# HGRN2 blocks half a period behind the RWKV blocks, in a two-layer encoder on one core

## The chip, the cores and the metric

One core of one Trainium2 chip. The metric is the device time of one execution, in microseconds; lower is better. Five engines work side by side, each through its own queue in order: TensorE (PE, matmuls), VectorE (DVE), ScalarE (ACT), GpSimd (POOL) and SyncE (SP, which issues all DMAs here).

## What is computed

Two layers over 2048 tokens of width 1024. The first mixes four HGRN2 heads ("a") and eight RWKV-7 heads of width 64 ("b"), the second is a convolution with an RG-LRU; each ends in a gated output projection and a layer norm.

```python
for l in range(DEPTH):
    mod = cond @ ada_w[l] + ada_b[l]
    shift, scale, gate = jnp.split(mod, 3, axis=-1)
    h = x * (1.0 + scale[:, None]) + shift[:, None]
    if l % 2 == 0:
        u = h @ ev_w_in[e]
        qA, fA, iA, gA, rB, kB, vB, zB, gB = jnp.split(u, EVEN_SPLITS, axis=-1)
        oA = hgrn2_chunkwise(qA, fA, iA, lbs[e], a_norm_g[e])
        oB, vf = rwkv7_mix(rB, kB, vB, zB, ...)
        mixed = jnp.concatenate([oA * jax.nn.silu(gA), oB * jax.nn.silu(gB)], axis=-1)
        y = mixed @ ev_w_out[e]
    else:
        ...
    x = layer_norm(DEEPNORM_ALPHA * x + (1.0 + gate[:, None]) * y, ln_g[l], ln_b[l])
```

The RWKV part is a scan with a state of 64x64 for each head:

```python
def step(S, inp):
    r_t, w_t, k_t, v_t, a_t, b_t = inp
    sa = jnp.einsum('bhvk,bhk->bhv', S, a_t)
    S = S * w_t[:, :, None, :] + sa[..., None] * b_t[:, :, None, :] + v_t[..., None] * k_t[:, :, None, :]
    return S, jnp.einsum('bhvk,bhk->bhv', S, r_t)
```

## The kernel before

The tokens go in two super-blocks of 1024, and each super-block through both layers. A projection is a product of 1024x128 weights with 2 x 512 tokens. Each factor is split in a high and a low part, so that every product is three matmuls (L431 to L433); the cast of the weights runs on ScalarE (L367), the low part on POOL (L368).

**mix0** (L1227) is the first layer's mixer, and the change lies in it. Its matmuls on TensorE come in an order that a small planner makes. One planner step is a quarter of a projection of 512 tokens, six matmuls. The generator `projections` gives these steps: the low-rank inputs, then for each of four groups g three RWKV and three HGRN2 projections, then the gates; it ends at step 272. The list `tasks` holds pairs of a due step and a generator. For each g and each half b of the super-block these are `rate_steps` (decay rates), `b_steps` (two RWKV heads over 512 tokens) at 40 + 48g + 24b, and `a_steps` (one HGRN2 head over the same tokens) at 64 + 48g + 24b. After each projection step every due task runs up to its next `yield n`, which makes it due n steps later. So a period is 24 steps, and in it one RWKV block and one HGRN2 block are woven into 24 steps of projections. This fixes TensorE's order only; the instructions of the other engines are put in order by a scheduler with priorities, and `tc.high_priority(offset=...)` puts some of them earlier.

**b_steps** has 8 chunks of 64 tokens in a block. In order:
- L857 to L894: normalised keys, decays, the products zr and bk;
- psc (L905, two groups of chunks) with its masks (L912, into the tile zb, called `sc` in the code): the score matrices;
- L918 and L921: the 16x16 diagonal blocks go out to DRAM and come back as ai, one block to a partition. L965 (POOL) writes the ones of the diagonal;
- pbn, pv, pk, pzt and pg: other products;
- L969 to L974 (VectorE): the inversion of the 16x16 triangles, 15 pairs of a multiplication and a sum; the result goes through DRAM again (L977, L980) into xd, and L984 transposes it into xn;
- plq (L994), pzq (L1004), plx (L1023) and pz (L1034): matmuls that join inverses of 16 into those of 64. Between pzq and plx stands a transposition on VectorE, xm (L1010), whose input ScalarE writes (L1008);
- pwv (L1049), pmq (L1063), and then the chain: pn (L1078), and for each of the eight chunks a pair of matmuls (L1087) with the state before, and a copy with decay on VectorE (L1090) that gives the next state. One chunk goes with each planner step;
- py and the group norm (pvr).

**a_steps** (L630) starts with a front: logarithms on ScalarE, then on VectorE L643, the scan L645, L647, L650 and the decay products L664 to L667; then the scores sc_a (L679), with L694 to put them into one tile, pk_a (L743), pst (L750), po_a and the normaliser pss_a (L785).

The block of a period and that of the next overlap: the chain of one RWKV block runs while the next block is inverted. `WO0` names the buffers of these blocks that hold the raw output weights when the blocks are through. `up` is the pool of the projections' outputs.

Of the kernel before, what the change touches and what calls it, by code (L numbers as in the profile page):

```python
# [31 lines left out]
INV_STEPS = 6  # L32
# [23 lines left out]
for _n, _w in VEC_FIELDS:  # L56
# [3 lines left out]
WO0 = (  # L60
    (1, "b_kk", 1), (1, "b_m1", 1), (1, "b_ep", 1), (3, "b_bk", 1), (1, "a_b", 1), (1, "a_e", 1), (1, "a_lf", 1),
    (1, "a_kz", 1), (2, "b_zg", 1), (2, "b_bkt", 1), (2, "b_sv", 2),
)
# [5 lines left out]
def tile_encoder(  # L69
# [19 lines left out]
    nc = tc.nc  # L89
# [10 lines left out]
    wp = ctx.enter_context(tc.tile_pool(name="wp", bufs=4))  # L100
    up = ctx.enter_context(tc.tile_pool(name="up", bufs=11))
    sp_ = ctx.enter_context(tc.tile_pool(name="sp", bufs=1))
# [741 lines left out]
    def b_steps(p, sb, b, us, sgi_of):  # L844
# [31 lines left out]
        lam = tp.tile([P, 8], F32, name=f"lam_{nm}", tag="b_lam", bufs=2)  # L876
# [21 lines left out]
        for c4 in range(2):  # L898
            yield (6, 2)[c4]
            pscs = [ps.tile([P, 4, P], F32, name=f"psc_{nm}_{hd}_{c4}", tag="tb", bufs=2) for hd in range(2)]  # L900
            for ci in range(4):
                for hd in range(2):
                    hs = slice(64 * hd, 64 * hd + 64)
                    c = c4 * 4 + ci
# [62 lines left out]
        for q in range(2):  # L967
            nc.gpsimd.memset(xt.rearrange("p n i -> p (n i)")[64 * q : 64 * q + 64, q:128:18], 1.0)
        for i in range(1, 16):  # L969
            n = i // 2 + 1  # L970
            pv_ = pr[:, 0 : n * (i + 1)].rearrange("p (n j) -> p n j", j=i + 1)
            av = ai[:, 0 : i + 1, i].rearrange("p (o j) -> p o j", o=1).broadcast_to([P, n, i + 1])
            nc.vector.tensor_mul(pv_, xt[:, 0:n, 0 : i + 1], av)
            nc.vector.tensor_reduce(out=xt[:, 0:n, i], in_=pv_, axis=AX.X, op=ALU.add)  # L974
        xd_dr = dram.tile([8, 8, 8, 2, 16], F32, name=f"xd_{nm}", tag="xd", bufs=2)
        for q in range(2):
# [9 lines left out]
        nc.gpsimd.tensor_copy(x32, xd)  # L986
        yield INV_STEPS

# [20 lines left out]
        xn = tp.tile([P, 8, 32], F32, name=f"xm_{nm}", tag="b_xn")  # L1009
        nc.vector.transpose(xn, x32)  # L1010
        tt = tt_tiles[tt_count[0] % 2]
        tt_count[0] += 1
        for hb in range(4):
            rs_ = slice(32 * hb, 32 * hb + 32)
            o_ = 32 * (hb % 2)
            nc.gpsimd.tensor_copy(tt[rs_, :, o_ : o_ + 32], x32[rs_])
        yield 2
        plx = ps.tile([P, 8, 32], F32, name=f"plx_{nm}", tag="tb", bufs=2)
# [65 lines left out]
        for c in range(8):  # L1084
            if states[c] is not None:
                for hd, hs in hds:
                    nc.tensor.matmul(  # L1087
                        pn[hs, c], sc[hs, 0, c, 0:64], states[c][hs], start=False, stop=True, skip_group_check=True
                    )
            nc.vector.tensor_scalar_mul(states[c + 1], pn[:, c], lam[:, c : c + 1])  # L1090
            yield 1
# [135 lines left out]
    def mix0(sb, hs, w_first):  # L1227
# [30 lines left out]
        for g in range(4):  # L1258
            for b in range(2):
                early = 4 if g == 3 and b else 0  # L1260
                tasks.append((34 + 48 * g + 24 * b - early, rate_steps(g, sb, b, lr, sgi_of)))
                tasks.append((40 + 48 * g + 24 * b - early, (g, b, b_steps, ub)))
                tasks.append((64 + 48 * g + 24 * b, (g, b, a_steps, ua)))

# [135 lines left out]
```

## Time and profile before

| | before |
|---|---|
| median of 3 runs | 2369.66 us (2367.89 to 2370.66) |
| profiled execution | 2367.25 us |
| its span | 2365.5 us |
| granted TensorE clock, mean | 0.969 of 2.4 GHz |
| TensorE busy | 2194.7 us (93%) |
| VectorE busy | 1455.6 us (62%) |
| ScalarE busy | 1264.6 us (53%) |
| POOL busy | 557.7 us (24%) |

TensorE's order is the program; where it has no work, an input is late. So the profile is read from TensorE's waits: which line waited, and which instruction of which engine it waited for. The granted clock is either 1.0 or 0.5 in a stretch (2.4 or 1.2 GHz), and a mean between the two says how much of a stretch ran at the lower. The first super-block's mixer runs from about 100 to 765 us, the second's from about 950 to 1575 us.

### The profile page before, as it was taken

The page shows a single profiled execution, that of the slowest core. Times are in us where ns is not written, and L with a number is a line of the kernel's source. Part 1 is how long each engine was busy: PE and PEld are TensorE (multiplying, and loading weights), DVE is VectorE, ACT ScalarE, POOL GpSimd, SP SyncE. Part 2 cuts the span into 40 slices and gives each one's busy share as a digit, 9 for nine tenths or more (in the row PEclk, how much of TensorE's full clock was granted, in tenths as well). Part 3 has the DMA queues.
Part 4 walks back from the last instruction along what each step waited for, and adds up shares of the span by engine and source line. Part 5 has one row for each costly group of instructions (what it writes and reads, how often), then busy time and mean ns, then how long its engine had stood idle before and what let it go on. Part 6 is the DMA issues. An engine that isn't in the chain of part 4 may idle for free. (4 is left out here: it accounts for less than half of the span.)

```text
span 2365.5 us, 45520 instructions
## 1 busy us (share of the span) xinstructions
PE 2194.7 (93%) x18400; PEld 1727.5 (73%) x18400; DVE 1455.6 (62%) x2697; ACT 1264.6 (53%) x2035; POOL 557.7 (24%) x586
## 2 busy tenths in 40 slices
PE   5989999999999999799999999899999999989998
PEld 4767777777777877577677777678777788767776
DVE  6546666667643678466675666436766556766366
ACT  4344655446666633445565456774467643666541
POOL 3311111212111322112111111112334331353321
PEclk7989999999999999899999999999999999999999
DMA  8210111111332637111111113326311564112652
GB/s 299 92 38 27 40 36 35 44 25 42 97 114 82 223 123 248 35 31 38 33 41 35 44 25 118 112 84 237 130 59 63 169 218 156 63 58 94 200 182 98
DMA packets 185938, 229.82 MB, mean 97 GB/s; under 512 B 65912, under 2 KB 99320, under 8 KB 185728
## 3 DMA queue, kind: packets, MB, share of 16 engines
q1 hardware_dynamic: 185728, 226.92, 30.1%
q8 instruction: 144, 2.36, 0.4%
q14 instruction: 66, 0.54, 0.1%
HBM read 175.46 MB, written 51.39 MB: 96 GB/s over the span
## 5 line engine op out<-in xcount | busy, mean ns | idle before, releaser
L431 PE MATMUL pp_g<-hl_h,wh_g 128*128 128x512 f32 x512 | 212.0, 414 | 4.0 <-ACT go L595 4.0
L433 PE MATMUL pp_g<-hh_h,wl_g 128*128 128x512 f32 x512 | 204.0, 398 | 4.0 <-POOL wl_g L368 4.0
L432 PE MATMUL pp_g<-hh_h,wh_g 128*128 128x512 f32 x512 | 204.4, 399 | 0.0
L368 POOL TENSOR_TENSOR wl_g<-raw_g,wh_g 128x512 fp32r<-128x512 f32 x64 | 97.5, 1528 | 349.9 <-ACT wh_g L367 307.8
L431 PE MATMUL po<-hl_wo,wh_mx 128*128 128x512 f32 x448 | 176.3, 393 | 4.0 <-DVE y L527 4.0
L433 PE MATMUL po<-hh_wo,wl_mx 128*128 128x512 f32 x448 | 175.4, 391 | 0.0
L432 PE MATMUL po<-hh_wo,wh_mx 128*128 128x512 f32 x448 | 174.9, 390 | 0.0
L431 PE MATMUL pp_b<-hl_h,wh_b 128*128 128x512 f32 x384 | 167.8, 437 | 5.1 <-ACT cr_b L838 5.1
L431 PE MATMUL pp_a<-hl_h,wh_a 128*128 128x512 f32 x384 | 168.9, 440 | 0.0
L432 PE MATMUL pp_b<-hh_h,wh_b 128*128 128x512 f32 x384 | 153.5, 400 | 0.0
L432 PE MATMUL pp_a<-hh_h,wh_a 128*128 128x512 f32 x384 | 153.4, 399 | 0.0
L433 PE MATMUL pp_a<-hh_h,wl_a 128*128 128x512 f32 x384 | 153.1, 399 | 0.0
L433 PE MATMUL pp_b<-hh_h,wl_b 128*128 128x512 f32 x384 | 152.7, 398 | 0.0
L368 POOL TENSOR_TENSOR wl_a<-raw_a,wh_a 128x512 fp32r<-128x512 f32 x48 | 66.9, 1402 | 329.0 <-ACT wh_a L367 329.0
L368 POOL TENSOR_TENSOR wl_mx<-raw_mx,wh_mx 128x512 fp32r<-128x512 f32 x64 | 80.8, 1268 | 255.7 <-ACT wh_mx L367 255.7
L368 POOL TENSOR_TENSOR wl_b<-raw_b,wh_b 128x512 fp32r<-128x512 f32 x48 | 67.4, 1409 | 269.1 <-ACT wh_b L367 260.0
L431 PEld LDWEIGHTS pp_g<-hl_h,wh_g 128*128 128x128 f32 x512 | 99.0, 193 | 27.8 <-ACT go L595 4.9
L433 PEld LDWEIGHTS pp_g<-hh_h,wl_g 128*128 128x128 f32 x512 | 99.0, 193 | 27.6 <-POOL wl_g L368 5.7
L587 DVE TENSOR_TENSOR go<-go,oi 128x512 f32<-128x512 f32 x64 | 45.9, 722 | 111.0 <-DMA oi<-o_dr 63.8
L432 PEld LDWEIGHTS pp_g<-hh_h,wh_g 128*128 128x128 f32 x512 | 99.4, 194 | 18.9
L433 PE MATMUL pp_c<-hh_h,wl_c 128*128 128x512 f32 x256 | 101.3, 397 | 11.0 <-POOL wl_c L368 9.6
L431 PE MATMUL pp_c<-hl_h,wh_c 128*128 128x512 f32 x256 | 101.6, 397 | 2.7 <-DVE hl_h L368 2.6
(355 smaller groups left out, 5677.8 us busy)
## 6 DMA issues: line engine op xcount, KB each, us to landing
adw<-in_ada_w_dram SPq DMA_DIRECT2D x96, 256.0 KB
oi<-o_dr SPq DMA_DIRECT2D x64, 256.0 KB
m_dr<-go SPq DMA_DIRECT2D x56, 256.0 KB
raw_b<-in_w_ev_dram SPq DMA_DIRECT2D x48, 256.0 KB
raw_a<-in_w_ev_dram SPq DMA_DIRECT2D x48, 256.0 KB
raw_g<-in_w_ev_dram SPq DMA_DIRECT2D x32, 256.0 KB
wo<-in_w_evo_dram SPq DMA_DIRECT2D x32, 256.0 KB
raw_mx<-m_dr SPq DMA_DIRECT2D x32, 256.0 KB
```

The costliest lines, as they stand in the source:

```text
L368: return (eng or nc.vector).tensor_tensor(out=lo, in0=src, in1=hi.bitcast(F32), op=ALU.subtract)
L431: nc.tensor.matmul(pt, ah, bl, start=first, stop=False)
L432: nc.tensor.matmul(pt, ah, bh, start=False, stop=False)
L433: nc.tensor.matmul(pt, al, bh, start=False, stop=last)
L587: nc.vector.tensor_mul(go[b], go[b], oi[b])
```

## The change

- `a_steps` are due 12 steps later, at 76 + 48g + 24b, half a period after where they were.
- `b_steps`: two steps more before plx (`yield 4`); xm and the chain's copies at high priority. The six steps that the inversion is given are now split, one before it, one after its ninth row, four behind it.
- the raw output weights go to buffers of the RWKV block only, since the last HGRN2 block still needs its own.
- 15 in place of 11 buffers for the projections' outputs, paid for with a smaller scratch (`dynamic_dma_scratch_size`).

```diff
-    (1, "b_kk", 1), (1, "b_m1", 1), (1, "b_ep", 1), (3, "b_bk", 1), (1, "a_b", 1), (1, "a_e", 1), (1, "a_lf", 1),
-    (1, "a_kz", 1), (2, "b_zg", 1), (2, "b_bkt", 1), (2, "b_sv", 2),
+    (1, "b_kk", 1), (1, "b_m1", 1), (1, "b_ep", 1), (3, "b_bk", 1), (2, "b_zg", 1), (2, "b_bkt", 1),
+    (2, "b_sv", 2), (2, "b_sv", 2), (1, "b_bv", 2), (1, "b_bv", 2),
...
-    up = ctx.enter_context(tc.tile_pool(name="up", bufs=11))
+    up = ctx.enter_context(tc.tile_pool(name="up", bufs=15))
...
+        yield 1
         for i in range(1, 16):
...
             nc.vector.tensor_reduce(out=xt[:, 0:n, i], in_=pv_, axis=AX.X, op=ALU.add)
+            if i == 9:
+                yield 1
...
-        yield INV_STEPS
+        yield INV_STEPS - 2
...
-        nc.vector.transpose(xn, x32)
+        with tc.high_priority(offset=300):
+            nc.vector.transpose(xn, x32)
...
-        yield 2
+        yield 4
         plx = ps.tile([P, 8, 32], F32, name=f"plx_{nm}", tag="tb", bufs=2)
...
-            nc.vector.tensor_scalar_mul(states[c + 1], pn[:, c], lam[:, c : c + 1])
+            with tc.high_priority(offset=300):
+                nc.vector.tensor_scalar_mul(states[c + 1], pn[:, c], lam[:, c : c + 1])
...
-                tasks.append((64 + 48 * g + 24 * b, (g, b, a_steps, ua)))
+                tasks.append((76 + 48 * g + 24 * b, (g, b, a_steps, ua)))
...
-    nc = bacc.Bacc("TRN2", target_bir_lowering=False, num_devices=1)
+    nc = bacc.Bacc("TRN2", target_bir_lowering=False, num_devices=1, dynamic_dma_scratch_size=1024)
```

Lines behind the inversion move by 3 to 5: L973 is L974 after, L974 is L975, L1010 is L1014, L1023 is L1027, L1087 is L1091, L1090 is L1095.

The order of VectorE before, in the second super-block, where the chain of one block (sb_b_1_1, the copies) meets the inversion of the next (pr_b_1_0); the numbers at the end of a name tell tiles apart:

```order
L1090 TENSOR_SCALAR sb_b_1_1_13005<-pn_b_1_1_13006,lam_b_1_1_11884 128x64
L912 TENSOR_TENSOR zb_b_1_0_12765<-psc_b_1_0_0_1_13027,bmask 128x512
L912 TENSOR_TENSOR zb_b_1_0_12765<-psc_b_1_0_1_1_13028,bmask 128x512
L1090 TENSOR_SCALAR sb_b_1_1_13005<-pn_b_1_1_13006,lam_b_1_1_11884 128x64 x2
L937 TENSOR_TENSOR b_bv_b_1_0_13092<-u_b_2_2_0_12514,pbn_b_1_0_13070 128x512
L1090 TENSOR_SCALAR sb_b_1_1_13005<-pn_b_1_1_13006,lam_b_1_1_11884 128x64 x2
L694 COPY_PREDICATED st_348<-lmask,sc_a_1_1_13113 64x4x8x4 x2
L694 COPY_PREDICATED st_348<-lmask,sc_a_1_1_13113 64x4x16x2 x2
L735 TENSOR_TENSOR a_kz_a_1_1_12676<-a_kz_a_1_1_12676,a_b_a_1_1_12674 128x4x64
L736 TENSOR_TENSOR u_a_1_1_11755<-u_a_1_1_11755,a_b_a_1_1_12674 128x4x64
L973 TENSOR_TENSOR pr_b_1_0_13230<-xt_b_1_0_13229,ai_b_1_0_13048 128x2
```

Copies 0 to 4 stand ahead of the first multiplication of the inversion (L973), with the score masks and the end of an HGRN2 block between them. The same place after, from copy 0 on:

```order
L1095 TENSOR_SCALAR sb_b_1_1_12941<-pn_b_1_1_12942,lam_b_1_1_11801 128x64
L937 TENSOR_TENSOR b_bv_b_1_0_13006<-u_b_2_2_0_12391,pbn_b_1_0_12984 128x512
L667 TENSOR_TENSOR w_a_1_1_12979<-w_a_1_1_12979,u_a_1_1_11682 128x8x32
L1095 TENSOR_SCALAR sb_b_1_1_12941<-pn_b_1_1_12942,lam_b_1_1_11801 128x64
L974 TENSOR_TENSOR pr_b_1_0_13144<-xt_b_1_0_13143,ai_b_1_0_12925 128x2
L1095 TENSOR_SCALAR sb_b_1_1_12941<-pn_b_1_1_12942,lam_b_1_1_11801 128x64
L975 TENSOR_REDUCE xt_b_1_0_13143<-pr_b_1_0_13144 128x1
L974 TENSOR_TENSOR pr_b_1_0_13144<-xt_b_1_0_13143,ai_b_1_0_12925 128x6
L975 TENSOR_REDUCE xt_b_1_0_13143<-pr_b_1_0_13144 128x2
L974 TENSOR_TENSOR pr_b_1_0_13144<-xt_b_1_0_13143,ai_b_1_0_12925 128x8
L975 TENSOR_REDUCE xt_b_1_0_13143<-pr_b_1_0_13144 128x2
```

The first multiplication (L974) now stands ahead of copy 2 (the third L1095), and the front of an HGRN2 block has passed already. A little further on in the same queue:

```order
L974 TENSOR_TENSOR pr_b_1_0_13144<-xt_b_1_0_13143,ai_b_1_0_12925 128x28
L975 TENSOR_REDUCE xt_b_1_0_13143<-pr_b_1_0_13144 128x4
L974 TENSOR_TENSOR pr_b_1_0_13144<-xt_b_1_0_13143,ai_b_1_0_12925 128x32
L975 TENSOR_REDUCE xt_b_1_0_13143<-pr_b_1_0_13144 128x4
L1095 TENSOR_SCALAR sb_b_1_1_12941<-pn_b_1_1_12942,lam_b_1_1_11801 128x64
```

Copy 3 stands behind the seventh pair. POOL's order at the same inversion before, with the memset of the diagonal (L965) between two low parts of weights:

```order
L368 TENSOR_TENSOR wl_a_2_1_13289<-raw_a_2_1_13286,wh_a_2_1_13288 128x512
L368 TENSOR_TENSOR wl_b_0_3_0_13540<-raw_b_0_3_0_13537,wh_b_0_3_0_13539 128x512
L965 MEMSET ai_b_1_0_13048 128x16
L368 TENSOR_TENSOR wl_b_0_3_1_13546<-raw_b_0_3_1_13543,wh_b_0_3_1_13545 128x512
L966 MEMSET xt_b_1_1_14089 128x128
```

And after:

```order
L368 TENSOR_TENSOR wl_a_2_0_13152<-raw_a_2_0_13149,wh_a_2_0_13151 128x512
L368 TENSOR_TENSOR wl_a_2_1_13158<-raw_a_2_1_13155,wh_a_2_1_13157 128x512
L965 MEMSET ai_b_1_0_12925 128x16
L368 TENSOR_TENSOR wl_b_0_3_0_13446<-raw_b_0_3_0_13443,wh_b_0_3_0_13445 128x512
L368 TENSOR_TENSOR wl_b_0_3_1_13452<-raw_b_0_3_1_13449,wh_b_0_3_1_13451 128x512
```

Of the two low parts of the projection b_0_3, one stood ahead of L965, and both stand behind it now. Last, VectorE at the transposition xm (L1010), before:

```order
L643 SCALAR_TENSOR_TENSOR a_lf_a_1_1_14384<-u_a_6_1_12887,a_e_a_1_1_14380 128x512
L645 SCALAR_TENSOR_TENSOR a_b_a_1_1_14386<-smask,a_lf_a_1_1_14384 128x512
L830 SCALAR_TENSOR_TENSOR u_b_2_3_1_14331<-pp_b_2_3_1_14262,vec,u_b_2_3_1_14331 128x511
L834 SCALAR_TENSOR_TENSOR u_b_2_3_1_14331<-cr_b_2_3_0_14230,vec,u_b_2_3_1_14331 128x1
L1010 STREAM_TRANSPOSE xm_b_1_1_14374<-x_b_1_1_14138 128x256
```

And after, where xm is L1014:

```order
L725 TENSOR_TENSOR u_a_1_1_11682<-u_a_1_1_11682,a_b_a_1_1_12969 128x512
L738 TENSOR_TENSOR dec_a_1_1_13497<-a_b_a_1_1_12969 128x4
L1122 SCALAR_TENSOR_TENSOR zb_b_1_1_11814<-py_b_1_1_13245,vec,zb_b_1_1_11814 128x512
L1123 SCALAR_TENSOR_TENSOR zb_b_1_1_11814<-zb_b_1_1_11814,vec,b_bv_b_1_1_12150 128x512
L1014 STREAM_TRANSPOSE xm_b_1_0_13433<-x_b_1_0_13223 128x256
```

The front of the HGRN2 block (L643, L645) stood ahead of xm; after, the end of the RWKV block before does (L1122 and L1123).

## Rows read from the trace of the kernel before

**Rows 1.** Stretches: us, busy per engine (instructions), granted clock, DMA share, GB/s; middles and tails.

```profile
190.00:612.00 422.00, 402.51 (x5017) 309.04 (x5012) 278.72 (x645) 229.25 (x426) 70.16 (x97) 0.98 0.13 37
612.00:765.00 153.00, 138.00 (x1461) 108.53 (x1460) 71.32 (x169) 98.75 (x153) 23.45 (x23) 0.93 0.35 103
...
1002.00:1427.00 425.00, 407.22 (x5119) 312.86 (x5118) 280.59 (x656) 233.86 (x431) 71.42 (x98) 0.99 0.14 37
1427.00:1575.00 148.00, 133.19 (x1445) 104.76 (x1445) 69.96 (x167) 93.21 (x147) 22.91 (x23) 0.92 0.33 99
```

**Rows 2.** TensorE's waits in the middles, first, then second: us in total, times, longest.

```profile
PE plx_b L1023 <- DVE xm_b L1010: 12.5, 5, 3.9
...
PE plx_b L1023 <- DVE xm_b L1010: 11.3, 5, 3.6
PE psc_b L905 <- DVE zb_b L912: 3.2, 6, 0.8
```

**Rows 3.** Timeline around one wait of plx: start, us, engine, line, operation, idle before.

```profile
1137.62 2.13 DVE L645 TENSOR_TENSOR_SCAN a_b_a<-smask,a_lf_a 128x512 f32<-128x512 bf16 x1
...
1138.09 1.08 ACT L1008 COPY x_b<-pzq_b 16x128 f32<-16x128 f32 x4
...
1141.48 0.43 DVE L1010 STREAM_TRANSPOSE xm_b<-x_b 128x256 f32<-128x256 f32 x1
...
1141.96 0.95 PE L1023 MATMUL plx_b<-xm_b,zb_b 32*32 32x32 f32 x32 [3.39 <-DVE xm_b L1010]
```

**Rows 4.** Stretches behind the wait of rows 3 and behind a wait of 1.63 us.

```profile
1142.20:1145.60 3.40, 3.40 (x35) 2.11 (x28) 1.76 (x4) 2.06 (x5) 0.12 (x1) 0.50 0.02 5
...
1070.00:1085.00 15.00, 13.73 (x168) 10.76 (x169) 12.42 (x27) 12.96 (x25) 2.70 (x7) 1.00 0.07 19
```

**Rows 5.** TensorE's waits in the second tail.

```profile
PE pst_a L750 <- ACT a_w_a L745: 3.3, 1, 3.3
PE sc_a L679 <- DVE w_a L667: 3.2, 1, 3.2
PE pwv_b L1049 <- ACT tt L1037: 3.0, 1, 3.0
PE plx_b L1023 <- DVE xm_b L1010: 2.7, 2, 1.9
...
PE pn_b L1087 <- DVE sb_b L1090: 0.9, 1, 0.9
```

**Rows 6.** Timeline of VectorE at one inversion in the second middle.

```profile
1240.25 1.29 DVE L912 TENSOR_TENSOR zb_b<-psc_b,bmask 128x512 f32<-128x512 f32 x2 [0.78 <-PE psc_b L905]
...
1253.29 0.15 DVE L973 TENSOR_TENSOR pr_b<-xt_b,ai_b 128x2 f32<-128x2 f32 x1
...
1253.67 0.17 DVE L973 TENSOR_TENSOR pr_b<-xt_b,ai_b 128x6 f32<-128x6 f32 x1
...
1256.44 1.30 DVE L973 TENSOR_TENSOR pr_b<-xt_b,ai_b 128x45 f32<-128x45 f32 x1
```

**Rows 7.** Instructions by line and shape on VectorE: busy us, mean ns, idle before.

```profile
L973 DVE TENSOR_TENSOR pr_b<-xt_b,ai_b 128x45 f32<-128x45 f32 x16 | 16.6, 1035 | 0.5
```

**Rows 8.** Timeline of POOL beside rows 6.

```profile
1250.20 1.27 POOL L368 TENSOR_TENSOR wl_b<-raw_b,wh_b 128x512 fp32r<-128x512 f32 x1 [16.67 <-ACT wh_b L367]
1251.42 0.13 POOL L965 MEMSET ai_b<- 128x16 f32 x1
1256.39 1.26 POOL L368 TENSOR_TENSOR wl_b<-raw_b,wh_b 128x512 fp32r<-128x512 f32 x1 [4.84 <-ACT wh_b L367]
```

**Rows 9.** Timeline of TensorE in a chain, before the inversion.

```profile
1173.01 0.33 PE L1087 MATMUL pn_b<-sb_b,zb_b 64*64 64x64 f32 x4
...
1174.86 0.33 PE L1087 MATMUL pn_b<-sb_b,zb_b 64*64 64x64 f32 x4
1175.12 1.12 PE L925 MATMUL pbn_b<-sgi,bones 128*128 128x512 f32 x2
...
1177.26 0.50 PE L431 MATMUL pp_b<-hl_h,wh_b 128*128 128x512 f32 x1
...
1182.51 1.02 PE L944 MATMUL pk_b<-ident,bk_b 64*128 64x64 f32 x16
```

## The prediction

> **What bounds the kernel now.** I read the table of stretches first [rows 1]. TensorE is busy for 2194.7 of 2365.5 us, so only what makes TensorE wait, or run at its lower clock, can move the time. The change touches mix0 alone, and there the table gives, for each super-block, a middle (six periods of 24 planner steps) and a tail (the last period and its drain). In the middles TensorE has 422.00 - 402.51 = 19.5 and 425.00 - 407.22 = 17.8 us without work, in the tails 15.0 and 14.8. The granted clock says the rest: 0.98 and 0.99 in the middles, 0.93 and 0.92 in the tails. A stretch at 0.5 loses half its length. The middles hold 13.6 and 10.2 us of such stretches, so 11.9 us lost in both; the tails lose 0.07 x 153 + 0.08 x 148 = 22.5 us.
>
> The waits say for what [rows 2, 5]. In the middles plx, the matmul behind the second transposition xm, waits 12.5 and 11.3 us, in five places each; in the second, psc, which needs a buffer back from the mask multiplication, adds 3.2 in six places. Smaller waits fill the rest. Two lines of the timeline show why [rows 3]: ScalarE has written the transposition's input at 1139.17, but VectorE has the front of the HGRN2 block in its queue, a scan of 2.13 us and three multiplications, and reaches L1010 only at 1141.48. The wait is 3.4 us, and behind it the clock is 0.50 for 3.4 us; behind a wait of 1.63 us it stays at 1.00 [rows 4]. So a long wait here costs half as much again.
>
> Sum before, to be replaced: middles 37.3 + 11.9 = 49.2 us (4.1 in each of 12 periods), tails 29.8 + 22.5 = 52.3 us. The two first blocks, before the middles, have the same TensorE order up to the first HGRN2 block, and I leave them as they are.
>
> **The change part by part.**
>
> *HGRN2 12 steps later; xm first; two steps more before plx.* In the new order the front of the HGRN2 block (L643 to L664) no longer stands between pzq and plx; xm follows the last two RWKV output instructions, and plx has two more quarter projections (2 x 1.59 us, from [rows 9]: 1.85 between two chain matmuls, less 0.26 for the pair itself) in front. What was 3.4 us late is then early by several us. I take all of plx's 23.8 us away. The waits of psc go too: in the new order its two groups are two steps away from pn and from the HGRN2 decay products. Between nothing and all of it, I take all, because xm's own work is 0.43 us [rows 3].
>
> *What is next: the state chain.* The chain pn -> copy -> pn of eight chunks has one copy on VectorE for each step. Before, copies 0 to 4 stand in VectorE's queue ahead of the small inversion of the next block, and its 30 instructions begin behind them. Now the first multiplication of the inversion stands ahead of copy 2, seven multiplication/sum pairs ahead of copy 3, three ahead of copy 4, and the rest with several HGRN2 decay instructions ahead of copies 5 and 6. High priority raised the copies, but not over these. VectorE works in order, so a multiplication that waits for its input holds the copy.
>
> When does that input come? Its chain is: last mask multiplication, eight stores, one load, POOL's L965. From the end of the mask multiplication for head 0 (1240.94, half of the pair at 1240.25 [rows 6]) to L965 it took 10.5 us [rows 8]; the change leaves this chain as it is. When does the chain need copy 2? Along TensorE from the end of the new psc (1.5 us ahead of that zero), by [rows 9]: two steps 2.93 (twelve matmuls in a row, somewhat less than twice 1.59), pn 1.0 (as pk), chain matmuls 0.26, pbn with pv 2.14 (1175.12 to 1177.26), step 1.59, 0.26, step 1.59, 0.26, pk 1.0, step 1.59: 12.6, so 11.1 us after zero.
>
> The first multiplication could go at 10.65. But POOL now has a low-part subtraction L368 right behind L965 (before, it stood ahead of it), and its cast is done by then: before, it let L368 start 9.3 us after the zero [rows 8]. Beside L368 the multiplication of 128x45 took 1.30 us, from 1256.44, when L368 ran from 1256.39; small ones alone take 0.15 to 0.17 [rows 6, 8]. So the first multiplication ends at about 11.9 and copy 2 at 12.2: TensorE waits 1.2 us. The six pairs that follow at 0.4 us each (1253.29 to 1253.67, [rows 6]) put copy 3 at 14.9, against a need of 12.3 + 1.85 = 14.1: a wait of 0.9 (1.0 with the semaphore). Copy 4 has the long step with pzt and pg in front and is on time. From there to copy 5 VectorE has five pairs and some eight HGRN2 instructions of 0.4 us, about 6.5 us from the end of the score matmul; this makes copy 5 late by about 1.8. With 0.4 for small ones: 4.35 us a period. The bounds: 0 where VectorE slips every copy in, and 7.2 where the second L368 falls on the pairs too and the clock falls (below).
>
> *The clock.* Two waits of 1.2 and 0.9 us within 3 us are between the wait of 1.63 that left the clock at 1.00 and that of 3.4 that halved it [rows 4]. I count a fall of 3.4 us (1.7 lost) in every second period: 0.85. Middles after: 12 x 5.2 = 62.4, which is 13 us more than before.
>
> *Tails.* The last HGRN2 block ends 12 steps later, beside the gate projections (which run to step 272), not further out. The tail's long waits [rows 5] come from the last RWKV and HGRN2 blocks being alone with little TensorE work between dependent steps. After: sc_a (3.2), pwv (3.0), pst (3.3) and plx (2.7) have their inputs ahead; new are pk_a behind L735, which now stands behind the bk products of the last RWKV block, at the price of sc_a, 3.2; the last normaliser sum pss_a behind a table load, at the price of pst, 3.3; and four late chain copies at the row's 0.9. Sum 10.1. Before, 11.2 us of clock were lost in each tail beside four waits of 1.9 to 3.3 us [rows 1, 5], 2.8 for each; two such waits remain, so about 5 us. Tails after: 2 x 15.1 = 30.2, a gain of 22 us. Bounds: 0 (a new long wait for each removed) to 40.
>
> *The rest at nothing.* Fifteen input tiles and the smaller scratch are space; no queue of POOL issues a DMA. The raw output weights take other buffers; their loads and the store of the last HGRN2 block now stand in another order on SP, ahead of out_proj, with the whole gate projection as cover; without it 1 to 2 us. Splitting the inversion's yield moves no matmul: between its pieces TensorE has nothing of this block.
>
> Sum: 13 - 22 = -9 against the profiled 2367.25 us; the median of the runs lies 2.4 above it, so 2369.66 - 9 = 2360 us.
>
> **The rivals.**
>
> *B: the multiplications are not held.* If the multiplication starts before L368, or POOL's cast is late, copy 2 is on time, copy 3 late by 0.9, copy 5 by 1.3, with 0.3 for small ones: 2.5 a period, 30 in all, -19 - 22 = -41: 2329 us. For it: POOL and VectorE are released at the same moment, since L965 frees both. Against it: L965 and L368 are neighbours on one queue, VectorE needs a semaphore in between, and before it was the multiplication that waited in 12 of 16 blocks (16.6 us in 16 [rows 7] is 12 of 1.30 and 4 of 0.25). The Trainium skill, "SBUF — State Buffer", section "Who interferes with whom", says that a VectorE instruction with two SBUF inputs and a GpSimd instruction that reads SBUF exclude each other for the whole instruction, and that issue order decides which blocks. By that rule the row of 1.30 us is an instruction that came second; one that comes first would cost nothing, and the time would be that of this rival.
>
> *C: the clock falls in every chain.* As forecast, but 1.7 us lost in all 12: 6.05 x 12 = 72.6, +23 - 22 = +1: 2371 us, no change to be measured. For it: the tails, where several waits lie close together, run at 0.92 [rows 1, 5]. Against it: a slower TensorE needs copy 5 later, which gives part back.
>
> *D: slower, the chain follows the inversion.* The place is copy 3 in each middle period. If the second L368 (15.5 us after zero before [rows 8]) comes before the seventh multiplication, that is before about 14.5, it holds a second multiplication: copy 3 is late by 2.2 instead of 0.9, every chain has more than 3 us of wait within 5 us, and the clock falls in each. 5.5 + 1.7 = 7.2 x 12 = 86.4, +37 - 22 = +15: 2385 us. The point is thus 1 us earlier than it was. For it: the casts follow the projections, and and the new period has less work between the two casts.
>
> **How the numbers follow.** Forecast 0.40, B 0.18, C 0.20, D 0.22. What a measurement of this kernel can tell from no change is about 0.2%, 4.7 us: 2365 to 2374. Faster: B and 0.32 of the forecast's own spread, 0.50. Same: 0.08 of the forecast and 0.13 of C, 0.21. Slower: D and 0.07 of C, 0.29. Range: from B's to D's time, 2328 to 2387; the forecast and C alone span 2350 to 2375.
>
> **What would show it.** In the changed trace: no wait of plx above 0.5 us; psc's 0.8 us waits gone; pn waiting for sb_b in about three places of each middle period, 1.2, 0.9 and 1.8 us, with a multiplication of over 1 us as the first of each inversion; the middles' idle time 50 to 55 us in place of 37.3; the tails' clock at 0.96 or 0.97. The prediction is wrong in its main step if pn's waits in the middles sum to under 15 us (then B or better) or if plx still waits. It is wrong on the tails if their idle time stays near 15 us each at a clock of 0.93.

## The result, and the profile after

The change makes the kernel slower: 2393.81 us median of 4 runs (2383.74, 2393.44, 2394.17, 2396.49) against 2368.77 us median of 4 runs of the kernel before, a ratio of 1.0094 (95% interval 1.0076 to 1.0112; the ratios here are estimates over all runs, so they need not be the quotient of two medians, 1.0106 in this case). The prediction was 2360 us, with a range up to 2387.

The profiled execution is the fastest of the four, 2383.74 us, 16.5 above the profiled one of before (2367.25). Its mean clock is 0.969, as before; the other three have 0.963 to 0.965, and (0.969 - 0.965) x 2390 is about 10 us, which is the step from 2383.74 to 2394. So the trace shows 16.5 of the 25 us; the rest stands in executions without a trace, and all that is known of it is their clock.

To place the 16.5 us, both traces are cut at the same matmuls: a middle from the first matmul of the projection of the second RWKV input in group 1 to the first gate projection, and a tail from there to the second output tile. The stretches first of before, then of after; the columns are the stretch, its length, busy time (and instructions) of PE, PEld, DVE, ACT and POOL, the granted clock, the DMA share and GB/s:

```profile
204.17:610.86 406.69, 388.06 (x4833) 297.02 (x4831) 264.32 (x619) 219.44 (x404) 67.41 (x95) 0.98 0.13 37
610.86:789.83 178.97, 163.07 (x1575) 128.92 (x1568) 88.46 (x193) 122.05 (x186) 31.79 (x30) 0.94 0.34 103
1020.66:1426.02 405.36, 388.52 (x4863) 297.53 (x4861) 265.07 (x627) 219.94 (x404) 67.67 (x95) 0.99 0.14 37
1426.02:1605.65 179.63, 163.88 (x1586) 129.83 (x1579) 88.35 (x193) 122.04 (x186) 30.80 (x30) 0.93 0.34 103
```

```profile
196.06:615.45 419.39, 391.27 (x4902) 300.12 (x4900) 259.55 (x621) 233.09 (x415) 60.48 (x95) 0.98 0.13 35
615.45:796.31 180.86, 165.47 (x1647) 132.21 (x1639) 98.38 (x205) 120.88 (x189) 31.08 (x30) 0.95 0.34 106
1023.14:1442.69 419.55, 391.53 (x4932) 301.26 (x4931) 260.16 (x629) 233.19 (x415) 60.54 (x95) 0.98 0.13 35
1442.69:1622.53 179.84, 165.37 (x1657) 132.26 (x1650) 97.81 (x205) 120.89 (x189) 30.14 (x30) 0.96 0.34 106
```

The middles are longer by 12.7 and 14.2 us, 27 in all. The tails are longer by 1.9 and 0.2. The parts ahead of the two middles are shorter by 8.1 and 4.0 us, since HGRN2 work has moved out of them: the counts of PE show some 70 more matmuls in each of the four stretches. In the middles TensorE now has 28.1 and 28.0 us without work, where it had 18.6 and 16.8. The waits of TensorE say for what; the columns are the line, what it waited for, us in all, how often, and the longest:

```profile
PE pn_b L1091 <- DVE sb_b L1095: 29.9, 17, 2.9
PE pzq_b L1007 <- ACT lq_b L1001: 14.1, 10, 1.6
PE plq_b L997 <- DVE xn_b L987: 13.0, 2, 6.9
...
PE pzt_b L955 <- ACT bkt_b L945: 10.1, 2, 5.2
PE pk_a L743 <- DVE a_kz_a L735: 7.3, 2, 3.7
PE po_a L774 <- DVE a_e_a L762: 6.9, 6, 1.2
```

The waits of plx and those of psc for zb [rows 2] are gone. In their place pn waits for the chain copy 29.9 us, pzq waits 14.1 us for a copy on ScalarE, and three smaller lines are new. (plq waits in the two first blocks, as before.)

**Where pn waits.** One meeting of chain and inversion in the second middle, first VectorE, then POOL, then TensorE; the columns are start, duration, engine, line, operation, output and inputs, and in brackets the idle time before and what ended it:

```profile
1189.19 0.16 DVE L974 TENSOR_TENSOR pr_b<-xt_b,ai_b 128x2 f32<-128x2 f32 x1 [3.82 <-POOL ai_b L965]
...
1189.64 0.88 DVE L974 TENSOR_TENSOR pr_b<-xt_b,ai_b 128x6 f32<-128x6 f32 x1
...
1192.47 0.94 DVE L974 TENSOR_TENSOR pr_b<-xt_b,ai_b 128x32 f32<-128x32 f32 x1
...
1193.55 0.27 DVE L1095 TENSOR_SCALAR sb_b<-pn_b,lam_b 128x64 f32<-128x64 f32 x1
```

```profile
1189.22 1.27 POOL L368 TENSOR_TENSOR wl_a<-raw_a,wh_a 128x512 fp32r<-128x512 f32 x1
1192.07 1.28 POOL L368 TENSOR_TENSOR wl_a<-raw_a,wh_a 128x512 fp32r<-128x512 f32 x1 [1.57 <-ACT wh_a L367]
```

```profile
1189.60 0.33 PE L1091 MATMUL pn_b<-sb_b,zb_b 64*64 64x64 f32 x4 [0.18 <-DVE xt_b L975]
...
1193.88 0.33 PE L1091 MATMUL pn_b<-sb_b,zb_b 64*64 64x64 f32 x4 [2.36 <-DVE sb_b L1095]
```

The first multiplication goes 0.03 us ahead of L368 and is not held (0.16), so copy 2, right behind it, makes TensorE wait 0.18 us only. The second is held by the first L368 (0.88 in place of 0.17), the seventh by the second L368 (0.94 in place of 0.21), and copy 3, queued behind it, makes TensorE wait 2.36 us. So it is in ten of the twelve inversions of the middles: the first multiplication leads L368 by 0.03 or 0.04 us and takes 0.16, and the second takes 0.88 to 0.96. In the other two L368 leads by 0.02 us, and the first takes 1.27 and 1.29. A later multiplication is held in all twelve (0.90 to 1.33), in ten of them ahead of copy 3, and in these ten TensorE waits 2.1 to 2.9 us for copy 3; in the other two it waits 1.2. This is where the Trainium skill, "SBUF — State Buffer", section "Who interferes with whom", agrees with the rows: of two instructions that exclude each other, the one that was issued later waits. (Whether the first multiplication put L368 off in turn, its 1.27 us do not show.)

**Where pzq waits.** ScalarE ahead of one such wait, and the wait on TensorE:

```profile
1210.51 1.28 ACT L819 ACT_TABLE_LOAD   x1
...
1213.30 1.28 ACT L666 ACT_TABLE_LOAD   x1 [0.80 <-DVE w_a L665]
...
1216.28 1.28 ACT L819 ACT_TABLE_LOAD   x1
...
1218.28 1.28 ACT L351 ACT_TABLE_LOAD   x1
...
1220.16 0.26 ACT L1001 COPY lq_b<-plq_b 128x128 f32<-128x128 f32 x1
```

```profile
1220.47 0.69 PE L1007 MATMUL pzq_b<-xd,lq_b 32*16 32x16 f32 x64 [1.49 <-ACT lq_b L1001]
```

L819 computes the two sigmoids of the decay rates. The exponentials of an HGRN2 block (L666) now stand between them, each function needs its table, and a load takes 1.28 us. The copy for pzq is queued behind. Over the whole kernel, first before, then after (a group's columns: count, busy us, mean ns):

```profile
L819 ACT ACT_TABLE_LOAD x16 | 20.5, 1283 | 0.3
```

```profile
L819 ACT ACT_TABLE_LOAD x26 | 33.4, 1283 | 0.5
...
L666 ACT ACT_TABLE_LOAD x16 | 20.5, 1283 | 8.1 <-DVE w_a L665 8.1
```

(L666 had 4 loads before; over all lines the kernel goes from 171 loads to 181.) For the middles the prediction did not read ScalarE's order.

### The profile page after: what moved, and what is told of

The parts are those of the page before. It is cut to its first block, busy times and chain, and to the rows that moved or that the text cites. A ratio compares the mean times of both kernels' runs of the same rounds, so it can differ in the third digit from the quotient of the medians.

```text
span 2382.0 us, 45521 instructions
## 1 busy us (share of the span) xinstructions
PE 2191.5 (92%) x18400; PEld 1729.3 (73%) x18400; DVE 1456.3 (61%) x2697; ACT 1283.9 (54%) x2045; POOL 543.0 (23%) x586
## 4 chain that ended last, share of the span: by engine, by line
PE 53%; DVE 21%; ACT 10%; DMA 7%; issue 5%; SPq 2%; POOL 1%; DVEq 0%; POOLq 0%; ACTq 0%
PE po L431 4%; PE po L433 4%; PE po L432 4%; DMA ai_b<-ad_b 3%; PE pp_g L431 3%; PE pp_g L432 3%; PE pp_g L433 3%; DVE pr_b L974 3%; PE pp_a L431 2%; PE pp_b L431 2%; PE pp_b L432 2%; PE pp_b L433 2%; PE pp_a L432 2%; PE pp_a L433 2%; DVE xc_c L1148 2%
## 5 line engine op out<-in xcount | busy, mean ns | idle before, releaser
L368 POOL TENSOR_TENSOR wl_g<-raw_g,wh_g 128x512 fp32r<-128x512 f32 x64 | 96.5, 1512 | 309.9 <-ACT wh_g L367 304.8
L368 POOL TENSOR_TENSOR wl_mx<-raw_mx,wh_mx 128x512 fp32r<-128x512 f32 x64 | 81.6, 1277 | 273.0 <-ACT wh_mx L367 214.2
L974 DVE TENSOR_TENSOR pr_b<-xt_b,ai_b 128x2 f32<-128x2 f32 (+14 forms) x240 | 80.9, 337 | 64.4 <-POOL ai_b L965 58.0
L432 PE MATMUL pp_c<-hh_h,wh_c 128*128 128x512 f32 x256 | 100.6, 393 | 0.0
```

The costliest lines, as they stand in the source:

```text
L368: return (eng or nc.vector).tensor_tensor(out=lo, in0=src, in1=hi.bitcast(F32), op=ALU.subtract)
L432: nc.tensor.matmul(pt, ah, bh, start=False, stop=False)
```

## The experiments

After the result three theories of the loss stood: that the chain copies stand behind the inversion in VectorE's queue, and it is held by POOL; that the parted sigmoids hold ScalarE; and, against the first, that copies put ahead only move the loss, since the inversion then starts later. The first runs tell these apart; each edit is on top of the changed kernel unless it says otherwise.

### Copies ahead of the inversion

The first multiplication of an inversion is issued only after the newest chain copy:

```diff
-            nc.vector.tensor_mul(pv_, xt[:, 0:n, 0 : i + 1], av)
+            if i == 1 and last_copy[0] is not None:
+                with tc.issue_after(last_copy[0]):
+                    nc.vector.tensor_mul(pv_, xt[:, 0:n, 0 : i + 1], av)
+            else:
+                nc.vector.tensor_mul(pv_, xt[:, 0:n, 0 : i + 1], av)
...
+                cp = nc.vector.tensor_scalar_mul(states[c + 1], pn[:, c], lam[:, c : c + 1])
+            last_copy[0] = cp.ins
```

> The changed kernel, but the first multiplication of each small inversion is put in VectorE's order behind the newest chain copy, so that copies 0 to 4 stand ahead of it, as they did before the change. Theory 1 (the copies that wait behind the inversion and its multiplications, with the falls of the clock behind them, are the largest part of the loss): pn's waits for its copy, 29.9 us in 17 places in the changed kernel, drop below 6 us, the middles' clock returns to 0.98 to 0.99, and the time falls by 25 to 40 us, to 2355 to 2370. Theory 2 (the extra loads of ScalarE's tables and the waits of pzq behind them): pzq's 14.1 us stay, and the time falls by less than 10 us. Theory 3 (what the chain gains the inversion loses, which starts later): plq then waits for xn in the middles, 1 to 3 us in each of 12 periods, and the time stays within 10 us of the changed kernel's 2394.

Measured: 2402.49 us, 1.0142 [1.0117, 1.0167] against before: slower than the change itself. The waits of its TensorE:

```profile
PE plq_b L1002 <- DVE xn_b L992: 77.8, 16, 9.5
...
PE pn_b L1096 <- DVE sb_b L1100: 0.8, 2, 0.4
```

The chain's 29.9 us are down to 0.8, and plq, behind the inversion, now waits in all 16 blocks: 64.8 us more. For this edit the last of the three holds: the wait moves. Why plq waits, VectorE's order shows:

```profile
1204.80 0.15 DVE L977 TENSOR_TENSOR pr_b<-xt_b,ai_b 128x2 f32<-128x2 f32 x1
```

In the middles six copies (0 to 5) now stand ahead of the first multiplication, one more than before the change, and it starts 18.9 to 22.2 us after the score masks' zero (1185.69 here), in place of 10.4 to 11.8 in the change. VectorE is not full there: in the 7.4 us ahead of 1200.09 it has three copies of 0.28 us and otherwise waits for pn. So this edit does not show that there is no room for both; an order between the two, with copy 2 or 3 ahead, was not tried.

### The two sigmoids side by side

```diff
-        for i, bias in enumerate(("w0", "a0")):
-            last = nc.scalar.activation(sgi[:, i], pws[i], AF.Sigmoid, bias=V(bias, p))
+        first = nc.scalar.activation(sgi[:, 0], pws[0], AF.Sigmoid, bias=V("w0", p))
+        with tc.issue_after(first.ins), tc.high_priority():
+            last = nc.scalar.activation(sgi[:, 1], pws[1], AF.Sigmoid, bias=V("a0", p))
```

> The changed kernel, but the two sigmoids of each rate step stand next to each other on ScalarE, so that no exponential of an HGRN2 block comes between them. Table loads in front of L819 and L666, 26 and 16 in the changed kernel against 16 and 4 before, should return to about 16 and 6. Theory 2 (the table loads delay lq, so that pzq waits): pzq's waits, 14.1 us in ten places, drop below 3 us, and the time falls by 10 to 20 us, to 2374 to 2384. Theory 1 (chain copies): a fall of at most 10 us, since pn's 29.9 us stay. If the plq result waits for ScalarE for another reason, pzq's waits stay above 8 us.

Measured: 2372.61 us, 1.0017 [1.0004, 1.0029]: 21.2 us less than the change. The waits of pzq are gone, the loads at the sigmoids are back at 16, and those at L666 are 6:

```profile
L818 ACT ACT_TABLE_LOAD x16 | 20.5, 1283 | 0.3
...
L666 ACT ACT_TABLE_LOAD x6 | 7.7, 1283 | 1.1 <-DVE w_a L665 1.1
```

So ScalarE's order is worth 21 us of the change's loss, the term that the prediction lacked. Between the profiled executions it is 14.6 us (2369.15 at a clock of 0.974): pzq's 14.1 are gone, while pn's waits, with those put down to the inversion's sums, go from 30.9 to 35.0, and pzt's 10.1 stay.

### Both orders

The two edits together.

> Both edits: copies ahead of the inversion, and the two sigmoids together. If both causes are real and stand one behind the other on TensorE's path, the gains add: 2340 to 2355, faster than the kernel before. If the waits replace one another (theory 3), it is no faster than the better of the two by more than 5 us, and stays above 2362.

Measured: 2404.43 us, 1.0151 [1.0128, 1.0174]; plq waits 75.4 us in 15 places. With the copies first, the inversion is late whatever ScalarE does; pzq's waits are gone with that edit alone, and the sigmoids' gain does not show.

### The diagonal on VectorE

POOL's L965 goes to VectorE. POOL's L368 then need not wait for it and can run before the inversion, and the first multiplication no longer waits for POOL to write the diagonal:

```diff
-        nc.gpsimd.memset(ai.rearrange("p s t -> p (s t)")[:, 0:256:17], 1.0)
+        nc.vector.memset(ai.rearrange("p s t -> p (s t)")[:, 0:256:17], 1.0)
```

> The changed kernel, but the ones on the diagonal of ai are written by VectorE in place of POOL, so that POOL's low parts (L368) are no longer queued behind that load. The first one then runs as soon as its cast is done, some 2 us before the inversion starts, and the multiplication of 128x6, 0.88 us beside it in the changed kernel, takes about 0.17. If POOL's hold on VectorE is what makes copy 3 late, pn's longest waits, 2.36 us in the middles, drop to 1.3 to 1.7, and the time falls by 8 to 20 us (with fewer falls of the clock). If only the order counts (the copies behind seven pairs), they stay above 2 us and the time within 6 us of 2394.

Measured: 2374.92 us, 1.0025 [1.0012, 1.0037]: 18.9 us less than the change. The same meeting as above, POOL, then VectorE, then TensorE:

```profile
1177.95 1.29 POOL L368 TENSOR_TENSOR wl_a<-raw_a,wh_a 128x512 fp32r<-128x512 f32 x1 [19.88 <-ACT wh_a L367]
1182.93 1.26 POOL L368 TENSOR_TENSOR wl_a<-raw_a,wh_a 128x512 fp32r<-128x512 f32 x1 [3.70 <-ACT wh_a L367]
```

```profile
1180.50 0.17 DVE L974 TENSOR_TENSOR pr_b<-xt_b,ai_b 128x6 f32<-128x6 f32 x1
...
1182.97 0.27 DVE L1095 TENSOR_SCALAR sb_b<-pn_b,lam_b 128x64 f32<-128x64 f32 x1
1183.16 1.12 DVE L974 TENSOR_TENSOR pr_b<-xt_b,ai_b 128x45 f32<-128x45 f32 x1
```

```profile
1183.30 0.33 PE L1091 MATMUL pn_b<-sb_b,zb_b 64*64 64x64 f32 x4 [0.92 <-DVE sb_b L1095]
```

The first L368 runs before the inversion, the second multiplication takes 0.17, and the one that is held comes behind copy 3, which is late by 0.92 in place of 2.36. So the hold decides 1.4 us of copy 3's 2.36, and the seven pairs in front of it the other 0.9. (The inversion starts 10.9 us after the masks' zero in both meetings; in all twelve of the middles the second multiplication now takes 0.16 or 0.17.) The chain's waits fall from 29.9 to 22.8, the longest from 2.9 to 1.7. The profiled execution is 6.7 us shorter (2377.06); the median falls by 18.9. The rest stands in executions without a trace, and goes with the clock: 0.971 to 0.974 in all ten executions of this kernel, against 0.963 to 0.965 in three of the change's four.

### Both remedies, and three priorities more

Sigmoids and diagonal together, and then with the state updates of the HGRN2 block, its L735 and the bkt copies ahead as well:

```diff
+        with tc.high_priority(offset=300):
             nc.vector.tensor_mul(v128(ke)[:, :, 0], v128(ke)[:, :, 0], end(1).broadcast_to([P, 4, 64]))
...
+        with tc.high_priority(offset=300):
             for j in range(3):
                 state_after(j)
...
+            with tc.high_priority(offset=300):
                 nc.scalar.copy(bkt[:, hd], pk)
```

> The changed kernel with the two edits that each took some 20 us off: the sigmoids of a rate step next to each other, and the diagonal's ones on VectorE. If the two causes are independent (pzq behind ScalarE's table loads, copy 3 behind the multiplications that POOL holds), their gains of 21.2 and 18.9 us add, but for the clock that both give back: 2348 to 2360, faster than the kernel before by 0.4 to 0.9%. If both had acted on the same lost time, 2365 to 2373.

> The same two edits, and high priority for the HGRN2 state updates (L762), for the decay product in front of pk_a (L735) and for the copies of bkt on ScalarE. po_a waits for L762 6.9 us in six places of the changed kernel; these should fall below 2 us, so 4 to 8 us less than with the two edits alone. pk_a's 7.3 us and pzt's 10.1 us stand in the tails, where the order hardly moves: they should stay above 10 us in sum. If the tails' waits move as well, 10 to 16 us less.

Measured: 2354.72 us, 0.9948 [0.9924, 0.9971], for the two; 2329.41 us, 0.9833 [0.9810, 0.9856], with the priorities. The two gains add up: 21.2 + 18.9 = 40.1, and 2393.81 - 2354.72 = 39.1. The priorities give 25.3 more, where I had expected 4 to 8, or 10 to 16 if the tails moved too. po_a's and pk_a's waits (6.9 and 7.3) are gone, pzt's 10.1 stays; by the cuts at the same matmuls the two tails are 12.4 us shorter in all than with the two edits alone and the two middles 9.4, and the tails' clock is 0.98 and 0.97 in place of 0.96 and 0.95. Which of the three priorities did it was not tried. What is left of the chain's waits is many short ones, at a clock of 0.975 in the profiled execution:

```profile
PE pn_b L1095 <- DVE sb_b L1099: 19.9, 22, 1.7
```

This is the fastest kernel of the study, and it keeps the change's own order of TensorE, the two steps ahead of plx included.

### The parts of the change one by one

The shift alone: the kernel before with HGRN2 blocks due 12 steps later, the raw output weights' buffers, 15 input tiles and the smaller scratch, but no step added, no priority and no split. And xm's priority alone, on the kernel before:

```diff
-                tasks.append((64 + 48 * g + 24 * b, (g, b, a_steps, ua)))
+                tasks.append((76 + 48 * g + 24 * b, (g, b, a_steps, ua)))
```

```diff
-        nc.vector.transpose(xn, x32)
+        with tc.high_priority(offset=300):
+            nc.vector.transpose(xn, x32)
```

> The kernel before with the half-period shift of the HGRN2 blocks alone (with the buffers that it needs), no priorities, no split of the inversion and plx still two steps behind pzq. In its order copies 0 to 2 stand ahead of the inversion, copy 3 behind six pairs. Theory A (the shift as such brings the new waits: chain copies behind the inversion and POOL's low parts, pzq behind ScalarE): the time is 2375 to 2400, near the changed kernel's, and pn waits 15 us or more. Theory B (the shift alone gains, and the two priorities and the split, which pull the inversion ahead of copy 2, do the harm): 2340 to 2362, pn's waits under 10 us, plx's gone.

> The kernel before with the high priority for the transposition xm alone. In its order xm moves by at most a few instructions and still stands behind the scan of the HGRN2 block, because priorities decide only between instructions that the scheduler takes to be ready. If that is right, plx keeps its 29.1 us of waits (25 to 30) and the time is within 6 us of 2369. If the priority moves xm to where its input is ready, plx's waits fall below 12 us and the time to 2340 to 2355.

Measured: the shift alone 2336.08 us, 0.9873 [0.9840, 0.9907]; xm's priority alone 2369.64 us, 1.0002 [0.9984, 1.0019]. Priority did not help xm: plx still waits 28.3 us in 13 places (29.1 in 14 before). The shift clears plx by itself. Its waits, in a trace of the slowest of its four executions (2349.14 at a clock of 0.965; the others, 2335 to 2337, have 0.971 and 0.972):

```profile
PE pn_b L1087 <- DVE sb_b L1090: 11.5, 8, 3.2
PE pzq_b L1004 <- ACT lq_b L998: 8.5, 3, 3.0
PE plx_b L1023 <- DVE dec_a L738: 7.7, 2, 4.0
...
PE plx_b L1023 <- DVE xm_b L1010: 2.7, 2, 1.3
```

What is left of plx is four waits in all, in the tails. So the change holds something that costs 58 us more than its own main part, and the candidates are the two steps before plx, the priorities and the split. (I had expected the priorities and the split to do the harm.)

### The two steps before plx

The change with its two extra steps taken away, and the shift alone with only these two steps added:

```diff
-        yield 4
+        yield 2
         plx = ps.tile([P, 8, 32], F32, name=f"plx_{nm}", tag="tb", bufs=2)
```

```diff
-        yield 2
+        yield 4
         plx = ps.tile([P, 8, 32], F32, name=f"plx_{nm}", tag="tb", bufs=2)
```

> The changed kernel with one number put back: two steps, not four, between pzq and plx. The chain then runs two steps earlier against the inversion of the next block. In VectorE's order copies 0 to 2 stand ahead of the first multiplication again and copy 3 behind six pairs; the two sigmoids are parted in 3 places, not 10. If these two steps are the whole difference between the shift alone (2336) and the change (2394), the time is 2330 to 2350, pn waits under 15 us and pzq under 9 us. If the priorities or the split do the harm, it stays above 2370.

> The kernel before with the shift and the four steps ahead of plx, without the priorities and without the split of the inversion. Its order on VectorE, ScalarE and POOL shows the same pattern as the changed kernel's (first multiplication ahead of copy 2, seven pairs ahead of copy 3, sigmoids parted in 10 places). If the two steps are the cause, it is as slow as the changed kernel: 2383 to 2400, pn waits 25 to 35 us, pzq 12 to 16. If the priorities or the split are, it is near the shift alone, 2335 to 2350.

Measured: the change without the two steps 2343.36 us, 0.9876 [0.9855, 0.9897]; the shift with them 2393.93 us, 1.0096 [1.0076, 1.0116], the time of the change (1.0094). So the two steps alone turn a gain of 1.2% into a loss of 1%: 50.4 us with the priorities and the split (2393.81 against 2343.36), 57.8 without them (2393.93 against 2336.08). The priorities and the split do nothing clear of the noise: 0.1 us with four steps, and with two 7.3 us slower, where the intervals overlap almost wholly (0.9876 and 0.9873). The long waits of the shift with four steps are those of the change, within 2 us a line:

```profile
PE pn_b L1087 <- DVE sb_b L1090: 31.9, 18, 2.9
PE pzq_b L1004 <- ACT lq_b L998: 14.0, 10, 1.8
...
PE pzt_b L955 <- ACT bkt_b L945: 10.1, 2, 5.2
```

And the meeting of chain and inversion on VectorE in the change without them:

```profile
1163.79 0.28 DVE L1095 TENSOR_SCALAR sb_b<-pn_b,lam_b 128x64 f32<-128x64 f32 x1 [1.56 <-PE pn_b L1091]
1165.87 0.16 DVE L974 TENSOR_TENSOR pr_b<-xt_b,ai_b 128x2 f32<-128x2 f32 x1 [1.80 <-POOL ai_b L965]
...
1167.80 0.27 DVE L1095 TENSOR_SCALAR sb_b<-pn_b,lam_b 128x64 f32<-128x64 f32 x1
...
1168.91 1.08 DVE L974 TENSOR_TENSOR pr_b<-xt_b,ai_b 128x45 f32<-128x45 f32 x1
```

The chain is two steps earlier against the next block, and copies 0 to 4 stand ahead of the inversion, as before the change. A copy stands 2 us ahead of the first multiplication here, VectorE still idles 1.8 us before it, the next copy goes behind five pairs in time, and the multiplication that is held (1.08) comes behind that. In the second middle pn waits 3.7 us in four places, against 14.6 in eight in the change.

The chain is not all of it. Without the two steps the middles have 15.6 and 6.9 us without work, in place of 28.1 and 28.0. Over the whole kernel pn's waits fall by 16.2 us, pzt's by 10.1, po_a's by 6.9, pzq's by 5.5 and pk_a's by 4.8, while plx waits 10.4 us in the tails and plq 3.6 more; the profiled executions are 38.5 us apart. The two steps move the order of all that stands behind plx, ScalarE's too: the loads at L819 are 19 without them, 26 with them.

### The remedies on the shift alone

The shift with sigmoids and the three priorities, and with the diagonal as well (edits as above):

> The shift alone, with the sigmoids of a rate step together and high priority for the HGRN2 state updates, the decay product ahead of pk_a and the copies of bkt. The shift alone still has pzq 8.5 us in three places (sigmoids parted) and, in its profile, 18.8 us of halved clock in the middles. Without the parted sigmoids pzq's waits should be under 2 us: 8 to 15 us less than 2336, so 2318 to 2330, faster than every kernel so far. If the halved clock in the first middle has another cause, 2330 to 2340.

> The same with the diagonal's ones on VectorE, so that POOL's low part is not queued behind the load of ai. In the shift alone pn waits 11.5 us in eight places for copies behind the multiplications. If POOL's hold is in them as in the changed kernel (18.9 us there), 5 to 12 us less than the kernel without it. If the copies have enough time anyway, within 4 us of it.

Measured: 2340.94 us, 0.9878 [0.9853, 0.9902], and 2337.73 us, 0.9855 [0.9834, 0.9875]. I expected 2318 to 2330 of the first, and was wrong: neither is clearly faster than the shift alone (0.9873), and the diagonal takes off 3.2 us, not the 5 to 12 that a hold by POOL would have cost here. pzq's 8.5 us are gone, but two waits in the tails have taken their place:

```profile
PE plx_b L1027 <- DVE xm_b L1014: 10.1, 2, 5.1
...
PE psc_b L908 <- ACT tt L1041: 4.5, 2, 2.3
```

plx's wait for xm was 2.7 and psc's for tt 1.2 in the shift alone: 7.4 + 3.3 = 10.7 us more. That these balance is an argument from the waits alone: the traced execution of the shift alone is its slowest, and the traced one here (2339.10) is 10 us below it. Which of the edits put VectorE's work ahead of the last block's xm was not tried.

## Why the prediction was wrong

**The step that failed** is "plx has two more quarter projections in front ... what was 3.4 us late is then early by several us". It took the two steps as slack for plx and gave them no price of their own. The shift alone removes the wait of plx in the middles; the two steps then buy nothing there, and they push all that comes behind plx, the state chain first, two steps further into the inversion of the next block. I did count copies 2 and 3 against the inversion, but for the change as a whole, and never asked what either part would do alone. No rival said so either. The runs put 50 to 58 us on this step, of which the chain's waits are 16 in the traces. The price is that of the other engines' orders as they stand: with the remedies, the kernel with the two steps (0.9833) is no slower than the shift with its remedies (0.9855).

In the sum, two terms failed. Measured as the prediction measured them, time without work plus clock loss (an estimate from the stretches above, whose clock has two digits), the middles cost 25 us more than before, not 13, and the tails 9 us less, not 22: +16 in place of -9, and the profiled executions are 16.5 us apart.

**The missing term** is ScalarE. The sum has VectorE's copies and POOL's holds, and nothing for ScalarE, whose order in the middles I did not read. Two waits for it are new: pzq's 14.1 us in the middles, which the sigmoids side by side remove, for 21.2 us of the median; and pzt's 10.1 in the tails, which they leave as it is. That the last normaliser sum would stand behind a table load I did say, for the tails, but I did not ask where else loads would move.

**The chain**, point by point. The input of the inversion: predicted 10.65 us after the masks' zero, measured 10.4 to 11.8. Copy 2: predicted late by 1.2, in the rows above by 0.18, because the first multiplication was issued ahead of L368, which was B's condition, and it held in ten of twelve; B's gain did not come with it, since the same L368 then held the second multiplication. Copy 3: predicted 0.9; it is 2.36, which is D's 2.2 by D's mechanism: the score masks' zero is at 1178.34 there, the second L368 comes 13.7 us after it, within D's 14.5, and it holds the seventh multiplication. Copy 5: predicted 1.8, did not come: behind copy 3 there are three waits in the twelve chains, 1.36 us at most. So the sum of 12 x 4.35 = 52.2 us of waits in the middles met a measured idle time of 28.1 + 28.0 = 56.1, but by compensation: 30.9 of it at most is the chain (29.9 + 1.0), and the rest is pzq's 14.1, po_a's 6.9 and smaller ones. A total that fits is no evidence for its terms.

**The middles** are 27 us longer by the cuts above: idle time 28.1 + 28.0 - 18.6 - 16.8 = 20.7 more, and 6.2 more busy time. **The tails** are 2 us longer, with some 70 matmuls more in each. Their time without work goes from 31.6 to 29.9 us in both together; what they gain is in the clock, which rises from 0.94 and 0.93 to 0.95 and 0.96. Their long waits did go (sc_a, pst, pwv, plx [rows 5]), and others of the same size came: pk_a 3.65, for which I had 3.2; pss_a 2.1, for which I had 3.3; and 4.93 of pzt, which I did not have. There ScalarE waits 6.26 us for the HGRN2 front, and the bkt copies stand behind that in its queue (of ScalarE):

```profile
1486.08 0.63 ACT L661 ACTIVATE w_a<-a_lf_a 128x512 f32<-128x512 f32 x1 [6.26 <-DVE a_lf_a L643]
...
1491.32 1.06 ACT L945 COPY bkt_b<-pk_b 128x512 f32<-128x512 f32 x2
```

"A new long wait for each removed" was the lower bound of the tails, and for the waits it is what happened.

**What was right**: plx's and psc's waits in the middles are gone; pn waits where the chain meets the inversion; the hold of a multiplication by L368 sets copy 3. D, the slower side, was right in the place and in the price of copy 3, in ten of twelve chains. It was not right in the sum: its 12 x 5.5 = 66 us of chain waits met 30.9 at most, and it had tails 13 us too good and nothing for ScalarE. That its 2385 us lie near the profiled 2383.74 is luck. In the meeting shown, the clock falls behind copy 3's wait, as D said, and in seven of the ten such meetings it stands at 0.50 within 2 us of the end of that wait:

```profile
1195.30:1198.70 3.40, 3.40 (x80) 3.32 (x78) 3.29 (x11) 1.06 (x5) 0.00 (x0) 0.50 0.07 22
```

(TensorE is busy in all of these 3.40 us, at 0.50.) That it is worse in the other three executions, at 0.963 to 0.965, stands open: no trace shows which waits fell there.

## What to carry to other kernels

Split a change into its parts and price each of them alone: slack that is added ahead of a wait moves everything behind it, and here two steps of it cost 50 to 58 us while the shift they came with was worth 32. When blocks are moved against each other, read the new order of every engine that serves the bound one, ScalarE's functions too: work of another function between two activations costs two table loads, 2.6 us, to all that is queued behind. And an order that puts one late consumer first makes the other wait for the first one's inputs as well, in an engine that works in order; here the wait moved (29.9 us at pn became 64.8 at plq).

## What the runs showed of the chip

Two things I had not expected. A multiplication of two SBUF operands is held by POOL's subtraction only if it comes second: with 0.03 or 0.04 us of lead it took 0.16 us, behind it 0.88 to 1.33 (0.15 to 0.24 unheld, by its size). The lead is no gain by itself where a second multiplication follows at once, since that one is held instead. And executions of one kernel differ by the clock: 2383.74 us at 0.969 and 2396.49 at 0.963 for the change, 2335.10 at 0.971 and 2349.14 at 0.965 for the shift alone, so one traced execution can stand well off its median: with the diagonal, waits of 7 us went in the trace, and the median fell by 19.
